# A two-block language-model kernel: gates with the activations stationary, the causal convolution in strips on TensorE, states in parts, and first loads on three queues beside matmuls on a tile of ones

## The chip, the core and the metric

The kernel runs on one core of a Trainium2 chip. The metric is the time of one execution on the device, in microseconds (us). Engines are named as in the profile: PE is TensorE (PEld its weight loads), DVE is VectorE, ACT is ScalarE, POOL is GpSimd and SP is SyncE, which only issues transfers here. SPq and ACTq are what these engines' sequencers do, mostly issuing DMAs.

## The reference

The input is one sequence of 256 tokens, width 1024, in float32. It passes four layers.

- Two hybrid layers. Each takes `z = rmsnorm(x) @ w_in` and splits it into a sliding-window attention (8 heads), a chunked retention (4 heads, with its own gate `rg`) and two output gates:

```python
ya = sliding_window_sink_attention(aq, ak, av, sinks) @ w_a
yb = (r * silu(rg)) @ w_b                      # r: the normed retention
mixed = jax.nn.sigmoid(ga) * ya + jax.nn.sigmoid(gb) * yb
x = x + mixed @ w_out
x = x + jnp.square(jax.nn.relu(rmsnorm(x) @ w_up)) @ w_down
```

- An even layer: block attention beside a multi-scale pooling, gated, then an output projection.
- An odd layer: an S5 state-space model (32 groups, 64 states) beside a gated convolution:

```python
g = a * jax.nn.sigmoid(gl)
c = causal depthwise convolution of g, 31 taps, 512 channels
conv_out = (silu(layernorm(c)) @ pw) * silu(gd)
return jnp.concatenate([ssm_out, conv_out], axis=-1) @ w_out
```

## The kernel before

**Weights.** All weight matrices are cut into chunks of 128 x 2048 numbers (1 MB) and packed in the order in which they are used. `fetch` issues the load of a chunk on SP into one of three `raw` buffers. ACT copies it to `hi` (rounded to fp32r), DVE computes `lo = raw - hi`; each half chunk of 1024 columns has its own `hi` and `lo`, five buffers of each. `chunk()` keeps two chunks prepared ahead. An activation is likewise held as a pair (`xh`, `xl`), and a product is three matmuls: hi x hi, hi x lo, lo x hi.

**Two forms of a projection.** `n_group` keeps a 128-token block of the activation stationary and streams 512 columns of weights; the result has tokens on the partitions. A group of 512 output columns takes two chunks of 24 matmuls. `t_pair` and `t_quad` keep 128 x 128 weights stationary and stream 256 tokens; the result has channels on the partitions, and a chunk takes 48 matmuls. Before, the queries, keys, values and `rg` use `n_group`; the output gates (`gate`), `ya`, `yb` and `xo` use `t_pair` or `t_quad`. `R = row(r)` spreads the token norms along the free axis for the gates.

**The mixer.** `gate` multiplies by `R` on DVE and takes tanh on ACT. Attention and retention steps are written between the gates. After `ya` and `yb`, each pair of row blocks is added up on DVE and split into `mh`, `ml`, which the matmuls of `xo` read.

**The odd layer.** The gated input `g` has channels on the partitions, four blocks of 128 (q = 0 to 3), with 30 columns of zeros ahead of the 256 tokens. `NPE = (0, 0, 23, 31)` says how many of the 31 taps of a block are done on PE, as matmuls with a diagonal matrix (`cdg`, made on ACT; results in `cq`); the others are multiply-adds of 128 x 256 on DVE (line 1317). `states(q)` turns the inputs of the state-space model (`vb`, in the four `sm` banks of PSUM) into states by rotations with `E`, two scans and rotations back, on DVE. `s5_outputs` copies the powers `pwc` into `Q`. `ys` then makes the model's outputs, with 32 output columns per matmul in four column groups. `layer_mean` (`mu`) needs the complete convolution `cv`; `gb` and `ga` are the products with `glu_w`, `pw` that of the convolution's branch, `yo` the last projection.

**What sets the order.** Each engine works off its own instructions in order. The order is made at build time by a list scheduler, which goes by the order in the program and its own model of durations; `tc.high_priority(-n)` moves what it holds back by about n instructions. A tile that takes over the place of another (same tag) waits until the last reader of the old one is done, wherever that stands in the program.

**The start.** SP issues, in this order, a first piece of chunk 0, the gains `pv`, `x` pair 0, and then pieces and pairs in turn. The first chunk is split in pieces of 512 columns.

Of the kernel before, what the change touches and what calls it, by code (L numbers as in the profile page):

```python
# [32 lines left out]
P = 128  # L33
D = 1024
# [11 lines left out]
LOWC, LOWS, LOWW, LOWX = 400, 1500, 250, 300  # L46

NPE = (0, 0, 23, 31)
# [8 lines left out]
def _layer_chunks(l):  # L57
# [7 lines left out]
    def nform(cols):  # L65
        for c in range(2):
            cs.append([("w_in", l, np.arange(k * P, k * P + P), cols) for k in range(4 * c, 4 * c + 4)])
# [88 lines left out]
def pack_weights(cs, inp):  # L156
# [3 lines left out]
    for blocks, n in zip(cs, w):  # L160
# [17 lines left out]
       ("glub", 8), ("dw", 4 * CONVK), ("lng", 4), ("lnb", 4), ("sinks", 16)]  # L178
# [8 lines left out]

def pack_vectors(inp):
    def v(a):
        return np.asarray(a, np.float32).reshape(-1, P).T  # L190

    cols = [v(inp["g_mix"]), v(inp["g_mlp"]), v(inp["g_final"]), v(inp["pre_norm_g_2"]), v(inp["post_norm_g_2"]),
            v(inp["e_pool_scale_2"]), v(inp["o_d_2"]), v(inp["o_glu_b_2"]),
            inp["o_dw_2"][0].reshape(CONVK, 4, P).transpose(2, 1, 0).reshape(P, 4 * CONVK),
            v(inp["o_ln_g_2"]), v(inp["o_ln_b_2"]),
            np.broadcast_to(inp["sinks"].reshape(1, 16), (P, 16))]
    return np.ascontiguousarray(np.concatenate(cols, axis=1))
# [16 lines left out]
_CT = [("ident", 128), ("mask0", 128), ("maske", 256), ("ecos", 64), ("esin", 64), ("blk", 128), ("icnt", 64)]  # L214
# [11 lines left out]
def tables():  # L226
# [42 lines left out]
    put("blk", blk)  # L269
    return t  # L270
# [5 lines left out]
def build(ctx, tc, w, xin, pv_in, ct_in, s5_in, pg_in, out, parts=(0, 1, "e", "o"), dbg=None):  # L276
# [33 lines left out]
    def fetch(pieces=None):  # L310
# [10 lines left out]
        for h in range(0, n, HW):  # L321
            hi = stream.tile([P, HW], F32R, name=f"hi{i}_{h}", tag="hi", bufs=NH)
            lo = stream.tile([P, HW], F32R, name=f"lo{i}_{h}", tag="lo", bufs=NH)
            m = min(HW, n - h)
            step = m if pieces is None else 512
            for c in range(0, m, step):
                s, rs = slice(c, c + step), slice(h + c, h + c + step)
                if pieces is not None:
                    nc.sync.dma_start(raw[:, rs], src[:, rs])
                    pieces((h + c) // 512)  # L330
                A.copy(hi[:, s], raw[:, rs])  # L331
                V.tensor_tensor(lo[:, s], raw[:, rs], hi[:, s].bitcast(F32), op=OP.subtract)  # L332
            his.append(hi)
            los.append(lo)
# [54 lines left out]

    def n_group(xh, xl, width=512, hook=None):  # L390

        b = [bank("acc", f"ng{t}") for t in range(NT)]
        if width == 512:
            for c in range(2):
                hi, lo = chunk()
                if c and hook:
                    hook()
                for kk in range(4):
                    k = 4 * c + kk
                    ws = slice(kk * 512, kk * 512 + 512)  # L400
                    for t in range(NT):
                        ts = slice(t * P, t * P + P)
                        f, e = k == 0, k == KT - 1
                        T.matmul(b[t], xh[:, k, ts], hi[:, ws], start=f, stop=False)  # L404
                        T.matmul(b[t], xh[:, k, ts], lo[:, ws], start=False, stop=False)  # L405
                        T.matmul(b[t], xl[:, k, ts], hi[:, ws], start=False, stop=e)  # L406
# [195 lines left out]
    def layer(l, xh, xl, norm, after_mixer, done):  # L602
# [37 lines left out]
        R = row(r)  # L640
# [101 lines left out]
        ga, gb = (phase[0].tile([P, KT, S], F32, name=n, tag="gate", bufs=2) for n in ("ga", "gb"))  # L742
# [47 lines left out]
        n2 = Norm(D)  # L790
        for p in range(4):
            b = t_pair("acc", "xo", mh, ml)
# [231 lines left out]
    def s5_scalars(pool, tmp):  # L1024
# [119 lines left out]
        pwc = pool.tile([P, 2 * L, 16, 16], F32, name="pwc")  # L1144
# [83 lines left out]
    def odd(pool, xh, xl, n, s5, tabs5):  # L1228
# [31 lines left out]
        def states(q):  # L1260
# [10 lines left out]
            m = pool.tile([P, 4, NC], F32, name="Mt", tag="Mt", bufs=1)  # L1271
            V.tensor_copy(m, mL[:, 4 * q:4 * q + 4, None].to_broadcast([P, 4, NC]))
            V.memset(m[:, :, 0:1], 0.0)
# [10 lines left out]
        GW = CONVK - 1 + S  # L1284
# [4 lines left out]
        V.memset(g[:, :, 0:CONVK - 1], 0.0)  # L1289

        def tap(q, k):
            return vec("dw", q * CONVK + k)

        for p in range(2):
# [7 lines left out]
            stt(g[:, 2 * p:2 * p + 2, CONVK - 1:], th, 1.0, a1, AD, M)  # L1302
# [7 lines left out]
            with tc.high_priority(-LOWC):  # L1310
                for q in (2 * p, 2 * p + 1):
                    for k in range(NPE[q], CONVK):
                        src = g[:, q, k:k + S]
                        if k == NPE[q]:
                            ts(cv[:, q, :], src, tap(q, k), None, M)
                        else:
                            stt(cv[:, q, :], src, tap(q, k), cv[:, q, :], M, AD)
# [4 lines left out]
        for q in range(4):  # L1322
            if NPE[q] == 0:
                continue
            b = bank("sm", "cq")
            for k in range(NPE[q]):
                dg = pool.tile([P, P], F32, name="cdg", tag="cdg", bufs=7)
                A.activation(dg, ident, AF.Copy, scale=tap(q, k))
                T.matmul(b[:, 0:S], dg, g[:, q, k:k + S], start=k == 0, stop=k == NPE[q] - 1)
            if NPE[q] == CONVK:  # L1330
                A.copy(cv[:, q, :], b[:, 0:S])
            else:
                with tc.high_priority(-LOWC):
                    tt(cv[:, q, :], cv[:, q, :], b[:, 0:S], AD)
# [150 lines left out]

    def x_pair(i):

        if i == 0:
            nc.sync.dma_start(pv[:, 0:NG], pv_in[:, 0:NG])
        if i in (0, 2, 4, 6):  # L1490
            p = i // 2
            nc.sync.dma_start(x[:, 2 * p:2 * p + 2, :], xin[:, 2 * p:2 * p + 2, :])
            split_pair(xh, xl, x, "g_mix", 0, p)
# [127 lines left out]
```

## Time and profile before

| | |
|---|---|
| median of 3 runs | 1061.71 us (1060.48 to 1061.8) |
| profiled execution | 1061.03 us, span 1059.2 us |
| busy in the span | PE 98%, PEld 88%, DVE 75%, ACT 53%, POOL 1% |
| mean granted PE clock | 0.997 of full speed |
| HBM read | 174.80 MB, 166 GB/s over the span |

The span runs from the first to the last instruction of the profiled execution; what is left of its time lies outside. Matmuls are pipelined, so an instruction's duration is longer than the interval to the next one. An fp32 matmul or transpose shows as two records. In a row of the timeline the bracket says how long the engine was idle before, and what it waited for.

### The profile page before, as it was taken

The page shows a single profiled execution, that of the slowest core. Times are in us where ns is not written, and L with a number is a line of the kernel's source. Part 1 is how long each engine was busy: PE and PEld are TensorE (multiplying, and loading weights), DVE is VectorE, ACT ScalarE, POOL GpSimd, SP SyncE. Part 2 cuts the span into 40 slices and gives each one's busy share as a digit, 9 for nine tenths or more (in the row PEclk, how much of TensorE's full clock was granted, in tenths as well). Part 3 has the DMA queues.
Part 4 walks back from the last instruction along what each step waited for, and adds up shares of the span by engine and source line. Part 5 has one row for each costly group of instructions (what it writes and reads, how often), then busy time and mean ns, then how long its engine had stood idle before and what let it go on. Part 6 is the DMA issues. An engine that isn't in the chain of part 4 may idle for free.

```text
span 1059.2 us, 17142 instructions
## 1 busy us (share of the span) xinstructions
PE 1037.1 (98%) x6904; PEld 927.1 (88%) x6904; DVE 791.6 (75%) x1402; ACT 564.1 (53%) x895; POOL 9.4 (1%) x10
## 2 busy tenths in 40 slices
PE   7999999999999999999999999999999999999996
PEld 5888999998888887888999988888878999999885
DVE  6767666786666659568656799976668795989985
ACT  6545644555454546446444554444466558465453
POOL 0000000000000000000000000000000001010000
PEclk9999999999999999999999999999999999999999
DMA  9654434555555455553535555555544354334021
GB/s 330 224 178 159 160 118 162 182 182 199 194 188 197 171 199 168 190 177 106 195 120 178 202 199 169 204 185 196 201 160 159 129 200 160 120 125 175 2 80 40
DMA packets 26719, 176.95 MB, mean 167 GB/s; under 512 B 3088, under 2 KB 3216, under 8 KB 6032
## 3 DMA queue, kind: packets, MB, share of 16 engines
q1 hardware_dynamic: 26064, 174.26, 47.5%
q0 software_dynamic: 288, 1.07, 0.3%
q8 instruction: 54, 0.88, 0.3%
q10 hardware_dynamic: 288, 0.52, 0.1%
q14 instruction: 25, 0.20, 0.1%
HBM read 174.80 MB, written 1.05 MB: 166 GB/s over the span
## 4 chain that ended last, share of the span: by engine, by line
PE 90%; DVE 6%; ACT 2%; issue 1%; DMA 0%; SPq 0%; DVEq 0%; ACTq 0%
PE up L810 11%; PE ng L406 6%; PE ng L404 6%; PE ng L405 6%; PE up L811 6%; PE dn L832 5%; PE dn L833 5%; PE dn L834 5%; PE gate L386 3%; PE gate L387 3%; PE gate L388 3%; DVE big L1019 2%; PE xo L386 1%; PE xo L387 1%; PE yb L388 1%; PE yb L386 1%
## 5 line engine op out<-in xcount | busy, mean ns | idle before, releaser
L332 DVE TENSOR_TENSOR lo<-raw,hi 128x1024 fp32r<-128x1024 f32 (+1 forms) x331 | 398.1, 1208 | 177.3 <-ACT hi L331 176.2
L331 ACT CAST hi<-raw 128x1024 fp32r<-128x1024 f32 (+1 forms) x331 | 341.6, 1038 | 307.5 <-PE dn L834 83.2
L810 PE MATMUL up<-xs,hi 128*128 128x512 f32 x512 | 181.9, 398 | 0.0
L811 PE MATMUL up<-xs,lo 128*128 128x256 f32 x512 | 143.5, 280 | 0.0
L810 PEld LDWEIGHTS up<-xs,hi 128*128 128x128 f32 x512 | 96.2, 188 | 23.3
L404 PE MATMUL ng<-hi,xs 128*128 128x512 f32 x272 | 108.4, 399 | 8.1 <-ACT xs L455 8.1
L405 PE MATMUL ng<-lo,xs 128*128 128x512 f32 x272 | 107.2, 394 | 0.0
L406 PE MATMUL ng<-hi,xs 128*128 128x512 f32 x272 | 106.8, 395 | 0.1
L832 PE MATMUL dn<-hi,uph 128*128 128x512 f32 x256 | 100.1, 391 | 0.0
L833 PE MATMUL dn<-lo,uph 128*128 128x512 f32 x256 | 99.9, 390 | 0.0
L834 PE MATMUL dn<-hi,upl 128*128 128x512 f32 x256 | 99.6, 389 | 0.0
L811 PEld LDWEIGHTS up<-xs,lo 128*128 128x128 f32 x512 | 96.6, 189 | 1.0
L386 PE MATMUL gate<-xs,hi 128*128 128x256 f32 x256 | 74.0, 289 | 0.0
L388 PE MATMUL gate<-xs,lo 128*128 128x256 f32 x256 | 72.4, 283 | 0.0
L387 PE MATMUL gate<-xs,hi 128*128 128x256 f32 x256 | 72.4, 283 | 0.0
L404 PEld LDWEIGHTS ng<-hi,xs 128*128 128x128 f32 x272 | 51.7, 190 | 18.9 <-ACT xs L455 8.6
L406 PEld LDWEIGHTS ng<-hi,xs 128*128 128x128 f32 x272 | 51.4, 190 | 11.8 <-DVE xs L456 1.0
L405 PEld LDWEIGHTS ng<-lo,xs 128*128 128x128 f32 x272 | 51.7, 190 | 10.5
L832 PEld LDWEIGHTS dn<-hi,uph 128*128 128x128 f32 x256 | 48.1, 188 | 10.5
L834 PEld LDWEIGHTS dn<-hi,upl 128*128 128x128 f32 x256 | 48.1, 188 | 10.2
L833 PEld LDWEIGHTS dn<-lo,uph 128*128 128x128 f32 x256 | 48.1, 188 | 8.9
L386 PEld LDWEIGHTS gate<-xs,hi 128*128 128x128 f32 x256 | 49.0, 191 | 2.4 <-issue 2.3
(384 smaller groups left out, 2128.9 us busy)
## 6 DMA issues: line engine op xcount, KB each, us to landing
raw<-w_dram SPq DMA_DIRECT2D x161, 1024.0 KB, 4.9
raw<-w_dram SPq DMA_DIRECT2D x9, 256.0 KB, 5.8
x<-x_dram SPq DMA_DIRECT2D x4, 256.0 KB, 5.9
ctm<-ct_dram SPq DMA_DIRECT2D x1, 640.0 KB, 10.1
sp<-s_dram POOLq DMA_DIRECT2D x1, 536.0 KB, 3.9
pg<-pg_dram POOLq DMA_DIRECT2D x1, 512.0 KB, 3.9
out_dram<-xn SPq DMA_DIRECT2D x2, 256.0 KB, 2.0
out_dram<-xn ACTq DMA_DIRECT2D x2, 256.0 KB, 2.1
```

Of the source, the lines that this page charges most:

```text
L331: A.copy(hi[:, s], raw[:, rs])
L332: V.tensor_tensor(lo[:, s], raw[:, rs], hi[:, s].bitcast(F32), op=OP.subtract)
L386: T.matmul(o, wh, xh, start=first, stop=False, skip_group_check=True)
L387: T.matmul(o, wh, xl, start=False, stop=False, skip_group_check=True)
L404: T.matmul(b[t], xh[:, k, ts], hi[:, ws], start=f, stop=False)
L405: T.matmul(b[t], xh[:, k, ts], lo[:, ws], start=False, stop=False)
L406: T.matmul(b[t], xl[:, k, ts], hi[:, ws], start=False, stop=e)
L810: T.matmul(bs[i], hi[:, ws], xs2[:, k], start=k == 0, stop=False, skip_group_check=True)
L811: T.matmul(bs[i][:, 1, :], lo[:, ws], xh2[:, k, :], start=False, stop=k == KT - 1, skip_group_check=True)
L832: T.matmul(accs[t][h], th[:, kk, tk], hi[:, ws], start=f, stop=False)
L833: T.matmul(accs[t][h], th[:, kk, tk], lo[:, ws], start=False, stop=False)
L834: T.matmul(accs[t][h], tl[:, kk, tk], hi[:, ws], start=False, stop=e)
```

## The change

1. In the two hybrid layers the gates, `ya` and `yb` use the form of `n_group`, through a new `n_half` that does one chunk. Their results have tokens on the partitions, so the norm is ACT's scale and `R` is dropped. The sum of the two branches is turned to channels by 16 transposes a layer (`mixed`). The first `xo` pair runs over row blocks in its outer loop.
2. The convolution is done on PE alone. `strip` copies `g`, 32 channels at a time, into `g4` by 16 DMAs for each pair of blocks: the partitions of one strip hold 32 channels at four shifts of 8 tokens. A matmul with 32 output columns then does four taps at once; `taps` builds its matrices on POOL. There are 8 x 4 matmuls for each block. `g4` takes the places of `pwc` and `E`.
3. `states` is called in four places, a mask copy in it moves from DVE to ACT and the memsets to POOL.
4. `x` is loaded from ACT's queue, the first part of `pv` from POOL's, the weights alone from SP's. DVE makes the first `hi`. PE does 12 matmuls on the tile of ones before its first work.

```diff
-LOWC, LOWS, LOWW, LOWX = 400, 1500, 250, 300
-NPE = (0, 0, 23, 31)
+LOWS, LOWW, LOWX = 1500, 250, 300
+NIDLE = 12
+KP = 8
...
-    for p in range(4):
-        pair("w_in", ga + 256 * p)
-    for p in range(4):
-        pair("w_in", gb + 256 * p)
+    for c0 in (ga, ga + 512, gb, gb + 512):
+        nform(np.arange(c0, c0 + 512))
...
-    for p in range(4):
-        pair("w_b", 256 * p)
+    for c0 in (0, 512):
+        nform(np.arange(c0, c0 + 512), "w_b")
...
-                A.copy(hi[:, s], raw[:, rs])
+                if pieces is not None and i + h + c == 0:
+                    V.tensor_copy(hi[:, s], raw[:, rs])
+                else:
+                    A.copy(hi[:, s], raw[:, rs])
...
+    def n_half(b, xh, xl, c, nk=KT):
+        hi, lo = chunk()
+        for kk in range(4):
+            k = 4 * c + kk
+            ws = slice(kk * 512, kk * 512 + 512)
+            for t in range(NT):
+                ts = slice(t * P, t * P + P)
+                f, e = k == 0, k == nk - 1
+                T.matmul(b[t], xh[:, k, ts], hi[:, ws], start=f, stop=False)
+                T.matmul(b[t], xh[:, k, ts], lo[:, ws], start=False, stop=False)
+                T.matmul(b[t], xl[:, k, ts], hi[:, ws], start=False, stop=e)
...
-        R = row(r)
...
-        def gate(o, p):
-            b = t_pair("acc", "gate", xh, xl)
-            s = o[:, 2 * p:2 * p + 2, :]
-            V.tensor_tensor(s, b, row2(R), op=OP.mult)
-            A.activation(s, s, AF.Tanh, scale=0.5)
+        def gate(o, i):
+            c = i // 2
+            if i % 2 == 0:
+                gates["b"] = [bank("acc", f"gate{t}") for t in range(NT)]
+            n_half(gates["b"], xh, xl, i % 2)
+            if i % 2:
+                for t in range(NT):
+                    A.activation(o[:, t, c * 512:c * 512 + 512], gates["b"][t], AF.Tanh, scale=rc(0, t))
...
         for c in range(2):
-            for p, b in enumerate(t_quad("acc", "ya", oTh, oTl)):
-                s = ga[:, 4 * c + 2 * p:4 * c + 2 * p + 2, :]
-                V.scalar_tensor_tensor(s, s, 1.0, b, op0=OP.add, op1=OP.mult)
+            cs = slice(c * 512, c * 512 + 512)
+            bs = [bank("acc", f"ya{t}") for t in range(NT)]
+            n_half(bs, oTh, oTl, 0, 4)
+            for t in range(NT):
+                V.scalar_tensor_tensor(ga[:, t, cs], ga[:, t, cs], 1.0, bs[t], op0=OP.add, op1=OP.mult)
         mh, ml, ms = twin("ms")
-        for p in range(4):
-            b = t_pair("acc", "yb", rTh, rTl)
-            s = gb[:, 2 * p:2 * p + 2, :]
-            V.scalar_tensor_tensor(s, s, 1.0, b, op0=OP.add, op1=OP.mult)
-            V.tensor_tensor(s, s, ga[:, 2 * p:2 * p + 2, :], op=OP.add)
-            split(mh[:, 2 * p:2 * p + 2, :], ml[:, 2 * p:2 * p + 2, :], s)
+        def mixed(c):
+            for t in range(NT):
+                b = bank("sm", "mt").rearrange("p (n q) -> p n q", q=P)
+                for n in range(4):
+                    k = 4 * c + n
+                    T.transpose(b[:, n, :], gb[:, t, k * P:k * P + P], ident)
+                tk = slice(t * P, t * P + P)
+                split(mh[:, 4 * c:4 * c + 4, tk], ml[:, 4 * c:4 * c + 4, tk], b)
+        for c in range(2):
+            cs = slice(c * 512, c * 512 + 512)
+            bs = [bank("acc", f"yb{t}") for t in range(NT)]
+            n_half(bs, rTh, rTl, 0)
+            if c:
+                mixed(0)
+            n_half(bs, rTh, rTl, 1)
+            for t in range(NT):
+                s = gb[:, t, cs]
+                V.scalar_tensor_tensor(s, s, 1.0, bs[t], op0=OP.add, op1=OP.mult)
+                V.tensor_tensor(s, s, ga[:, t, cs], op=OP.add)
+        mixed(1)
...
-            b = t_pair("acc", "xo", mh, ml)
+            b = t_pair("acc", "xo", mh, ml, k_outer=p == 0)
...
+        def strip(p):
+            g4[p] = s5["pool"].tile([P, 2, 4, GS + 1], F32, name="g4", tag=("pwc", "E")[p], bufs=1)
+            for s in range(4):
+                for r in range(4):
+                    nc.sync.dma_start(g4[p][32 * s:32 * s + 32, :, r, 0:GS],
+                                      g[32 * r:32 * r + 32, 2 * p:2 * p + 2, KP * s:KP * s + GS])
+        def taps(q, h):
+            n = 2 * KP
+            o = PVO["dw"] + (2 * q + h) * n
+            tap[q, h] = pool.tile([P, n, 32], F32, name="taps", tag="taps", bufs=3)
+            G.tensor_tensor(tap[q, h], pv[:, o:o + n, None].to_broadcast([P, n, 32]),
+                            C("e32")[:, None, :].to_broadcast([P, n, 32]), op=M)
+        def convolve(p):
+            b = bank("sm", "cq").rearrange("p (j t) -> p j t", j=2)
+            for j in range(2):
+                q = 2 * p + j
+                for k in range(KP):
+                    if k % 4 == 0:
+                        taps(q, k // 4)
+                    for r in range(4):
+                        T.matmul(b[32 * r:32 * r + 32, j, :], tap[q, k // 4][:, 4 * (k % 4) + r, :],
+                                 g4[p][:, j, r, k:k + S], start=k == 0, stop=k == KP - 1)
+            A.copy(cv[:, 2 * p:2 * p + 2, :], b)
...
+            strip(p)
             if p == 0:
                 inputs()
                 with tc.high_priority(-LOWW):
-                    for q in range(4):
-                        states(q)
                     Q = s5_outputs(pool, s5)
...
-        for d in (gc, gd):
+        for i, d in enumerate((gc, gd)):
+            with tc.high_priority(-LOWW):
+                states(i)
             for p in range(2):
                 silu_gate(d[:, 2 * p:2 * p + 2, :], t_pair("acc", "og", xh, xl), R, 0.25)
...
+        convolve(0)
+        states(2)
+        convolve(1)
+        states(3)
...
+    nc.gpsimd.dma_start(pv[:, 0:NG], pv_in[:, 0:NG])
+    for p in range(4):
+        nc.scalar.dma_start(x[:, 2 * p:2 * p + 2, :], xin[:, 2 * p:2 * p + 2, :])
+    idle = bank("sm", "idle")
+    for _ in range(NIDLE):
+        T.matmul(idle[:, 0:P], ones, ones, start=True, stop=True)
```

## Rows read from the trace of the kernel before

**Rows 1.** The page's part 4, the chain that ended last, by engine.

```profile
PE 90%; DVE 6%; ACT 2%; issue 1%; DMA 0%; SPq 0%; DVEq 0%; ACTq 0%
```

**Rows 2.** Windows, busy us (x instructions) of PE, PEld, DVE, ACT, POOL; clock, DMA.

```profile
995.00:1008.00 13.00, 10.26 (x293) 8.91 (x293) 12.98 (x30) 0.62 (x1) 0.00 (x0) 1.00 0.01 3
```

**Rows 3.** Timeline of PE, odd layer: start, us, what, [idle before <- releaser].

```profile
996.50 1.97 PE L1368 MATMUL ys<-wall,Q 128*32 128x63 f32 x128
...
1002.85 1.36 PE L1348 MATMUL mu<-big,ones 128*128 128x256 f32 x4
1006.95 1.13 PE L1348 MATMUL mu<-big,ones 128*128 128x256 f32 x4 [2.74 <-DVE big L1010]
...
1035.35 0.36 PE L387 MATMUL pw<-is__10046,hi 128*128 128x256 f32 x1
```

**Rows 4.** Timeline of all engines, the first 21 us.

```profile
0.73 1.28 ACT L331 ACT_TABLE_LOAD   x1 [0.73 <-PEq L1611]
...
0.84 0.17 DVE L349 MEMSET ones<- 128x128 f32 x1 [0.84 <-PEq L1611]
...
1.65 0.42 SPq L1492 DMA_DIRECT2D x<-x_dram  x1
...
6.71 0.91 ACT L455 ACTIVATE xs<-x,pv 128x256 fp32r<-128x256 f32 x2 [1.95 <-DMA x<-x_dram]
...
7.27 0.80 PE L404 MATMUL ng<-hi,xs 128*128 128x512 f32 x1 [7.27 <-ACT xs L455]
...
13.58 0.40 PE L406 MATMUL ng<-hi,xs 128*128 128x512 f32 x1
...
20.40 0.39 PE L406 MATMUL ng<-hi,xs 128*128 128x512 f32 x1
```

**Rows 5.** The chain in order of time: start, us on the chain, what.

```profile
11.91 0.43 PE ng L405
...
32.18 0.87 PE tp L560 x8
...
66.62 0.45 PE rb L534 x4
...
100.50 0.12 PE gate L386
...
104.09 0.12 PE gate L386
```

**Rows 6.** Timeline at the end of the first mixer.

```profile
194.90 0.28 PE L388 MATMUL yb<-rTs,lo 128*128 128x256 f32 x1
...
199.04 0.69 DVE L450 TENSOR_TENSOR ms<-gb,ms 128x512 fp32r<-128x512 f32 x1 [0.69 <-ACT ms L449]
```

**Rows 7.** Windows of the start (last columns: clock, DMA share, GB/s).

```profile
0.00:7.20 7.20, 0.00 (x0) 0.00 (x0) 0.86 (x2) 2.39 (x4) 0.21 (x4) 1.00 0.63 145
7.20:12.10 4.90, 4.83 (x11) 3.84 (x12) 4.34 (x8) 4.65 (x11) 0.00 (x0) 1.00 1.00 351
```

**Rows 8.** DMA issues: count, KB each, median us from issue to landing.

```profile
raw<-w_dram SPq DMA_DIRECT2D x161, 1024.0 KB, 4.9
...
sp<-s_dram POOLq DMA_DIRECT2D x1, 536.0 KB, 3.9
...
out_dram<-xn SPq DMA_DIRECT2D x2, 256.0 KB, 2.0
```

**Rows 9.** The tile `cq`: durations in ns, first and last start.

```profile
L1329 PE MATMUL cq<-big,cdg x108: 377/378/380, 970.7 to 993.8; 128*128 128x256 f32 x108
```

**Rows 10.** Timelines of POOL, ACT and DVE in the odd layer.

```profile
937.49 3.57 POOL L1221 MEMSET Q<- 128x2048 f32 x2
...
950.24 0.41 ACT L1175 ACTIVATE Q<-pwc 64x256 f32<-64x256 f32 x1
...
978.76 0.42 DVE L1019 SCALAR_TENSOR_TENSOR wall<-wall,tb 128x256 f32<-128x256 f32 x1
...
979.75 18.29 DVE L1019 SCALAR_TENSOR_TENSOR big<-big,pv 128x256 f32<-128x256 f32 x46
```

More of the change, by code (lines that the diff above doesn't have):

```diff
@@ L63, in _layer_chunks, with nform @@
                             for b in range(4)])
-    def nform(cols):
+    def nform(cols, name="w_in"):
         for c in range(2):
-            cs.append([("w_in", l, np.arange(k * P, k * P + P), cols) for k in range(4 * c, 4 * c + 4)])
+            cs.append([(name, l, np.arange(k * P, k * P + P), cols) for k in range(4 * c, 4 * c + 4)])
     def pair(name, c0, n=1024):
@@ L185, with strips @@
 NG = 16
+def strips(dw):
+    t = np.zeros((4 * KP, 512), np.float32)
+    t[:CONVK] = dw
+    return t.reshape(4, KP, 4, 4, 32).transpose(0, 4, 2, 1, 3).reshape(P, 16 * KP)
 def pack_vectors(inp):
@@ L193, in pack_vectors @@
             v(inp["e_pool_scale_2"]), v(inp["o_d_2"]), v(inp["o_glu_b_2"]),
-            inp["o_dw_2"][0].reshape(CONVK, 4, P).transpose(2, 1, 0).reshape(P, 4 * CONVK),
+            strips(inp["o_dw_2"][0]),
             v(inp["o_ln_g_2"]), v(inp["o_ln_b_2"]),
@@ L269, in tables @@
     put("blk", blk)
+    put("e32", np.tile(np.eye(32), (4, 1)))
     return t
@@ L393, in n_group @@
         if width == 512:
[L394 to L406, printed above, removed]
+            n_half(b, xh, xl, 0)
+            if hook:
+                hook()
+            n_half(b, xh, xl, 1)
         else:
@@ L739, in ret_flip @@
                 split(rTh[:, 4 * c:4 * c + 4, tk], rTl[:, 4 * c:4 * c + 4, tk], b)
-        ga, gb = (phase[0].tile([P, KT, S], F32, name=n, tag="gate", bufs=2) for n in ("ga", "gb"))
-        def gate(o, p):
-            b = t_pair("acc", "gate", xh, xl)
-            s = o[:, 2 * p:2 * p + 2, :]
-            V.tensor_tensor(s, b, row2(R), op=OP.mult)
-            A.activation(s, s, AF.Tanh, scale=0.5)
+        ga, gb = (phase[0].tile([P, NT, D], F32, name=n, tag="gate", bufs=2) for n in ("ga", "gb"))
+        gates = {}
+        def gate(o, i):
[6 more added lines that the diff above has]
+                    A.activation(o[:, t, c * 512:c * 512 + 512], gates["b"][t], AF.Tanh, scale=rc(0, t))
         ret_gate(0)
@@ L1143, in s5_scalars @@
         pwb = pool.tile([P, 2 * L, 16, 16], F32, name="pwb", tag="pwb", bufs=1)
-        pwc = pool.tile([P, 2 * L, 16, 16], F32, name="pwc")
+        pwc = pool.tile([P, 2 * L, 16, 16], F32, name="pwc", tag="pwc", bufs=1)
         for pw, src, first in ((pwb, 0, (fr, fi)), (pwc, 2, (ar, ai))):
@@ L1270, in states @@
             tt(wt[:, 1], wt[:, 1], tb[:, 0], SU)
-            m = pool.tile([P, 4, NC], F32, name="Mt", tag="Mt", bufs=1)
-            V.tensor_copy(m, mL[:, 4 * q:4 * q + 4, None].to_broadcast([P, 4, NC]))
-            V.memset(m[:, :, 0:1], 0.0)
+            m = w2("Mt")[:, 0:4 * NC].rearrange("p (r c) -> p r c", r=4)
+            A.copy(m, mL[:, 4 * q:4 * q + 4, None].to_broadcast([P, 4, NC]))
+            G.memset(m[:, :, 0:1], 0.0)
             mf = m.rearrange("p r c -> p (r c)")
@@ L1281, in states @@
             stt(wt[:, 1], wt[:, 1], -1.0, tb[:, 0], M, SU)
-        GW = CONVK - 1 + S
+        GW = 4 * KP + S
         big = pool.tile([P, 4 * (GW + 3 * S)], F32, name="big", tag="big", bufs=1)
@@ L1288, in odd @@
                       for i in range(3))
-        V.memset(g[:, :, 0:CONVK - 1], 0.0)
-        def tap(q, k):
-            return vec("dw", q * CONVK + k)
+        G.memset(g[:, :, 0:CONVK - 1], 0.0)
+        G.memset(g[:, :, CONVK - 1 + S:], 0.0)
+        GS = S + KP - 1
+        g4, tap = {}, {}
+        def strip(p):
[21 more added lines that the diff above has]
+            A.copy(cv[:, 2 * p:2 * p + 2, :], b)
         for p in range(2):
@@ L1305, in odd @@
                 with tc.high_priority(-LOWW):
-                    for q in range(4):
-                        states(q)
                     Q = s5_outputs(pool, s5)
                 G.dma_start(pg, bass.AP(tensor=pg_in.tensor, offset=pg_in.offset, ap=[[0, P], [1, D]]))
[L1310 to L1317, printed above, removed]
-        for d in (gc, gd):
+        for i, d in enumerate((gc, gd)):
+            with tc.high_priority(-LOWW):
+                states(i)
             for p in range(2):
                 silu_gate(d[:, 2 * p:2 * p + 2, :], t_pair("acc", "og", xh, xl), R, 0.25)
[L1322 to L1334, printed above, removed]
+        convolve(0)
+        states(2)
+        convolve(1)
+        states(3)
         fh, fl, fs = twin("fs")
```

12 lines of the change are left out of this document (4 added, 8 removed).

## The prediction

> **What bounds the kernel now.** I read the page's chain first, then the windows, then the timeline and the chain where they leave TensorE. PE holds 90% of the chain, DVE 6% [rows 1]: a microsecond taken out of PE's queue is one off the time wherever PE does not wait. The windows show where it does: from 995 to 1008 DVE is full and PE is not [rows 2]. PE's timeline names that wait, 2.74 us before the second part of the mean over channels (`mu`), for DVE, which still has taps of the convolution to do [rows 3]. The other place is the start: nothing runs on PE for 7.27 us [rows 4], and the matmuls after it come at half pace. So there are three stretches, each with its own sum, against the profiled execution: a span of 1059.2 us and a time of 1061.0, 0.7 under the median of 1061.7.
>
> **The two mixer layers.** Gates, `ya` and `yb` change from 48 matmuls of 256 columns to 24 of 512 for each 1 MB chunk of weights. In a gate 30 intervals between matmuls take 3.59 us, 0.1197 each [rows 5]; in an `n_group`, the form they change to, 30 intervals take 6.82 us (13.58 to 20.40), 0.2273 each [rows 4]. A chunk falls from 48 x 0.1197 = 5.75 to 24 x 0.2273 = 5.46 us, 0.29 less. There are 16 gate chunks, 4 of `ya` and 8 of `yb`: 28 x 0.29 = 8.2 us. The row `R` of each layer goes: 2 x 0.45 = 0.9 us [rows 5]. What is added is `mixed`: 16 transposes a layer. One transpose is two records; eight records take 0.87 us [rows 5], so one takes 0.217 and 32 take 7.0 us. Net 8.2 + 0.9 - 7.0 = 2.1 us of PE work saved.
>
> DVE loses eight 128x512 multiplications a layer, and ACT's tanh reads PSUM instead; neither ends a wait of PE there, so I count nothing. The splits stay as many.
>
> The transposes also lengthen the last chain of the mixer. Now the last `yb` matmul starts at 194.90 and the last subtraction behind it ends at 199.73, 4.6 us after the matmul's end [rows 6]; PE does `xo` matmuls meanwhile and loses about half a microsecond. After, there are two more DVE operations of 0.69 us, four transposes (0.87) and one more handover: some 2.4 us more, 7.0 us. Token tile 0 ends 0.7 us earlier, the 24 `xo` matmuls of the first four row blocks cover 2.9, and the eight transposes are work themselves (1.7): at most 1.7 us stays, nothing if matmuls of the next `xo` pair are drawn ahead, and the old half microsecond goes. I take 0.5 a layer. If PE keeps the written order (transposes ahead of `xo`), it idles for four DVE operations less the 0.7, and a weight's `lo` (some 1.2) among them: 3.3 us a layer. Layers: 2.1 - 1.0 = **1.1 us saved**, between 2.1 saved and 4.5 lost.
>
> **The start.** Now `x` pair 0 is issued at 1.65, behind a weight piece and `pv` on SP; the activation that waits for it begins at 6.71, the first matmul at 7.27 [rows 4]. After, it is first on ACT's queue, at about 0.74, where the table load stands now. That load (1.28 us) follows the four issues and is over by 3.7: nothing waits for it. With the same 5 us to land, the activation begins near 5.7 and a matmul near 6.2. The tile of ones is ready at 1.0 [rows 4]. Twelve fp32 matmuls of 128 columns take 12 x 0.217 x 1.89 = 4.9 us at the slow pace and end at 6.1: no obstacle. 1.89 is the ratio of a 512-column interval early, 0.43 us [rows 5], to 0.2273 later: the 1.2 GHz level after an idle stretch against 2.4, though the windows' clock column reads 1.00 [rows 7]. PE reached the higher level 4.9 us after its first matmul. If it does so again, the real ones start fast near 6.1, and about 11 of them save 0.2 us each, 2.3 in all. Earlier start and clock: 1.1 + 2.3 = 3.4 us.
>
> Then supply: from 7.2 to 12.1 the DMA engines are full at 351 GB/s, but before 7.2 they moved 145 [rows 7]. If they are full from 2.7 us on, (7.2 - 2.7) x 0.351 = 1.58 MB land by 7.2 instead of 1.04: 0.54 MB, 1.5 us earlier. So the start gives between 1.5 (all supply) and 3.4 us; nothing is seen of PE waiting for weights there, so it has some slack, and I take **2.8 us**. POOL's issue of `pv` is not shown; the nearest row, `sp` on POOL, lands 3.9 us after issue [rows 8], before `x`.
>
> The Trainium skill ("DMA: Bandwidth & Descriptors", section "Issuing engines are not separate DMA queues") speaks against this part: transfers issued from several engines share the same 16 DMA engines, and only issue time is saved. The full engines of [rows 7] agree; if supply alone counts, the start gives the 1.5 us and the total is 1047.8.
>
> **The convolution.** Now 54 diagonal matmuls (108 records, first start 970.7, last 993.8) take 0.216 us a record, 0.432 a matmul, 23.3 us in all [rows 9]; DVE does the other 70 taps at 0.40 us, 28 us [rows 10]. After, PE does everything in 128 matmuls of 32 output columns each, in four column groups. Their cost is the largest unknown. If the groups overlap fully, one costs 0.432 / 4 = 0.108 and all 13.8 us. The nearest row is `ys`, also fp32, 32 columns wide and in four groups: 128 records take 1.97 us [rows 3], less the last one's own 0.22, 0.0138 each, 0.0276 a matmul of 63 moving columns. A wide one would take 0.432 x 63/256 = 0.106, so the overlap is 3.85-fold. Scaled to 256 columns that is 0.112 and 14.4 us. I take 14.2: 9.1 us off PE. From above: no overlap, 0.432 each and 55.3 us.
>
> The Trainium skill ("TensorE: Matmul & The Clock Gate", Part 3 on packing small matmuls) gives less: 2.38-fold for three column groups. An estimate at that share for four is 3.17-fold, 17.4 us for the convolution and 1049.7 in the sum; the 3.85 of `ys` is better than that.
>
> With the taps gone the wait before `mu` goes: 2.74 us, 3.0 with the drained pipe. What is late next? The strips. Those of pair 1 take `E`'s place and so wait for the last of the four `states`, which ends on DVE at 979.2 now [rows 10]. Seven taps that lie before it (2.8 us) and its copies and memsets (about 1 us) are gone, so about 975. Sixteen issues on SP at 0.42 us [rows 4] and a landing of 2.0 (the output's, [rows 8]) give 983.7. PE comes to the second half of the convolution at 970.7 + 7.1 = 977.8, or after `ys` (8.8 us, from 994 to 1002.85 in [rows 3]) at 986.6. If the convolution is put first, it waits up to 5.9 us; if `ys`, nothing. I take 1.5. The strips of pair 0 wait for the last read of `pwc`, by the `Q` copies that end at 950.7 [rows 10]; PE needs them 20 us later. Weights queue behind these 32 issues on SP, 6.7 us a pair; they are issued some two chunks, 11 us, ahead and land in 4.9 [rows 8], so this is hidden. Without that cover it costs up to 5 us. POOL builds eight tap tiles of 512 elements: two memsets of 2048 take it 3.57 us [rows 10], so 0.45 us from below and, with two inputs beside the output, 1.4 from above; PE uses a tile for 16 x 0.111 = 1.8 us, and three are ready ahead. Nothing.
>
> The chain from `mu` to the second half of `pw` (1007 to 1035 in [rows 3]) is as long as PE's work beside it: it moves with `mu` and is not shortened. Odd block: 9.1 + 3.0 - 1.5 = **10.6 us**.
>
> Sum: 1.1 + 2.8 + 10.6 = 14.5; 1061.0 - 14.5 = **1046.5 us**.
>
> **The rivals.** (1) *Late handovers.* PE waits for strips (5.9 instead of 1.5) or keeps the written order in the layers (6.6 instead of 1.0): 1050.9 or 1052.1, both 1056.5; a held-up weight queue is of the same size. For it: PE takes its queue in an order fixed ahead of the run. Against: before [rows 6]'s subtraction ended, `xo` matmuls had already been drawn ahead. (2) *Partial overlap.* With the groups overlapping three-fold, 55.3 / 3 = 18.4 us: 1050.7. Two by two, 0.216 a matmul and 27.6 us, 4.3 more than now: 1061.0 + 4.3 - 3.0 + 1.5 - 3.9 = 1059.9. Against: `ys`. (3) *No overlap,* the slower side: 55.3 us, 32.0 more, and no time lost to strips: 1061.0 + 32.0 - 3.0 - 3.9 = 1086.1. It decides from (23.3 + 3.0 + 3.9) / 128 = 0.236 us a matmul on. For it: no row has 256 columns in a 32-column group. (4) *Supply,* three queues that give only their earlier start: 1047.8.
>
> **How the numbers follow.** Forecast 0.42; (4) 0.18: both within the forecast's own range, 1041 to 1050. (1) 0.22 and three-fold overlap 0.05, 1050 to 1057. Two by two 0.05. (3) 0.05. Something unseen 0.03, most of it slower. The range 1040 to 1057 leaves out about 0.13. A change under 0.2% (2.1 us) can't be told from none, and two by two lies on that edge: same 0.05, faster 0.88, slower 0.07.
>
> **What would show it.** Right: the first 512-column matmul near 6.2 us and 0.23 us apart; gate chunks of 5.46 us; `cq` records 0.055 us apart on average and no wait for DVE before `mu`; `gb` near 995. Wrong: `cq` records at 0.1 or more; a gap before the second half of `cq`; PE idle between the last `yb` and `xo`; PE waiting for weights near 17 to 24 us.

## The result and the profile after

The changed kernel takes 1068.83 us (median of 4 runs) beside 1061.1 us of the kernel before on the same chip. The ratio is 1.0071, with an interval of 1.0052 to 1.0089: slower, where 1046.5 was forecast and the range ended at 1057. The profiled execution has a span of 1066.4 us [before: 1059.2] and a mean granted clock of 0.985 [0.997].

The page's chain has become purer: VectorE's share falls from 6% to 2% [rows 1]. But a share says what ends last, not how long it takes.

```profile
PE 93%; DVE 2%; ACT 2%; issue 1%; DMA 1%; SPq 1%; DVEq 0%; ACTq 0%; POOLq 0%
```

The first landmarks show where to look. Matmuls of a given tile start, after less before: the first transposes -0.2 us, the second layer -2.9, the even layer's `pu` -4.5, the first diagonal or packed convolution matmul -1.4, the first `gb` +7.4. So the loss lies in the odd block: 3.1 us between `pu` and the convolution and 8.8 between its first half and `gb`. The windows of the second stretch stand beside [rows 2]: the wait for VectorE that stood in 995 to 1008 is gone, and 21 us ahead of it TensorE is busy for 3.

```profile
974.00:995.00 21.00, 3.16 (x51) 1.55 (x41) 11.10 (x16) 0.59 (x1) 4.07 (x3) 0.65 0.32 95
995.00:1008.00 13.00, 13.00 (x203) 8.04 (x205) 0.00 (x0) 0.59 (x1) 1.06 (x1) 0.90 0.03 7
```

TensorE's timeline (beside [rows 3] and [rows 9]) names the wait: the second half of the convolution waits 17.84 us for the strips of pair 1. It then starts at a granted clock of 0.50 (994.3 to 996 us), the 1.2 GHz level; over the two windows above it is 0.65 and 0.90.

```profile
969.29 7.14 PE L1353 MATMUL cq<-g,taps 128*32 128x256 f32 x128
994.27 1.65 PE L1353 MATMUL cq<-g,taps 128*32 128x256 f32 x4 [17.84 <-DMA g<-big]
...
998.32 7.11 PE L1353 MATMUL cq<-g,taps 128*32 128x256 f32 x122
...
1013.50 1.99 PE L1394 MATMUL mu<-big,ones 128*128 128x256 f32 x8
```

The timelines of SP and VectorE (beside [rows 10]) show why the strips are late. SP issues those of pair 0 from 949.20, and those of pair 1 only from 984.43, 0.03 us after VectorE's last product that reads `E`. Each 16 issues take 10.2 to 11.1 us, 0.64 to 0.69 each.

```profile
949.20 11.08 SPq L1335 DMA_DIRECT2D g<-big  x16
984.43 10.17 SPq L1335 DMA_DIRECT2D g<-big  x16
...
973.74 2.92 DVE L1312 TENSOR_TENSOR_SCAN wall<-Mt,wall 128x256 f32<-128x256 f32 x2
983.71 0.69 DVE L1046 TENSOR_TENSOR wall<-wall,E 128x512 f32<-128x512 f32 x1
984.78 0.42 DVE L1055 SCALAR_TENSOR_TENSOR wall<-wall,tb 128x256 f32<-128x256 f32 x1
```

At the start (beside [rows 4]) the four `x` issues stand at 0.74 on ScalarE's queue, but the first real matmul comes at 7.87, 0.6 later than before. The table load waits until `x` has landed, and the activation behind it then waits for `pv`, which GpSimd's queue delivers at 7.3. The ones matmuls end at 5.52; after the 2.35 us without work the real ones run 0.42 apart, and the window that stands beside [rows 7] has a clock of 0.65.

```profile
0.74 2.13 ACTq L1535 DMA_DIRECT2D x<-x_dram  x4
1.06 4.46 PE L1538 MATMUL idle<-ones 128*128 128x128 f32 x24 [1.06 <-DVE ones L358]
1.24 0.72 POOL L1533 DMA_DIRECT2D pv<-pv_dram  x1 [0.79 <-POOLq L1660]
5.32 1.28 ACT L468 ACT_TABLE_LOAD   x1 [5.32 <-DMA x<-x_dram]
7.31 0.91 ACT L468 ACTIVATE xs<-x,pv 128x256 fp32r<-128x256 f32 x2 [0.70 <-DMA pv<-pv_dram]
7.87 0.79 PE L408 MATMUL ng<-hi,xs 128*128 128x512 f32 x1 [2.35 <-ACT xs L468]
```

```profile
7.20:12.10 4.90, 4.23 (x12) 3.37 (x13) 4.23 (x9) 4.79 (x11) 0.00 (x0) 0.65 1.07 401
```

One more place stood in no plan. At the entry of the odd block TensorE runs dry twice in the short matmuls of `kb`, with nothing to wait for ("issue"), and `su` starts at 0.21 us a matmul instead of 0.12, at a granted clock of 0.50 from 902 to 904 us, the 1.2 GHz level. From the first `kb` matmul to the first `cb` matmul behind `su` it takes 12.29 us, before 8.24: 4.05 us are lost here.

```profile
895.50 1.30 PE L1241 MATMUL kb<-cd,BA 128*32 128x32 f32 x128
898.01 1.29 PE L1241 MATMUL kb<-cd,BA 128*32 128x32 f32 x128 [1.22 <-issue]
902.01 0.37 PE L395 MATMUL su<-xs,hi 128*128 128x256 f32 x1 [2.72 <-issue]
```

### The profile page after: what moved, and what is told of

It reads as the page before. It is cut to its first block, busy times and chain, and to the rows that moved or that the text cites. A ratio compares the mean times of both kernels' runs of the same rounds, so it can differ in the third digit from the quotient of the medians.

```text
span 1066.4 us, 16107 instructions
## 1 busy us (share of the span) xinstructions
PE 1029.9 (97%) x6428; PEld 887.8 (83%) x6428; DVE 760.1 (71%) x1307; ACT 546.6 (51%) x843; POOL 23.3 (2%) x25
## 3 DMA queue, kind: packets, MB, share of 16 engines
HBM read 174.82 MB, written 1.05 MB: 165 GB/s over the span
## 4 chain that ended last, share of the span: by engine, by line
PE 93%; DVE 2%; ACT 2%; issue 1%; DMA 1%; SPq 1%; DVEq 0%; ACTq 0%; POOLq 0%
PE up L846 11%; PE ng L410 6%; PE ng L408 6%; PE ng L409 6%; PE up L847 6%; PE dn L869 5%; PE dn L868 5%; PE dn L870 5%; PE gate L408 3%; PE gate L409 3%; PE gate L410 3%; PE xo L395 1%; PE xo L397 1%; PE xo L396 1%; PE yb L409 1%; PE yb L410 1%
## 5 line engine op out<-in xcount | busy, mean ns | idle before, releaser
L870 PEld LDWEIGHTS dn<-hi,upl 128*128 128x128 f32 x256 | 48.1, 188 | 10.2
L408 PE MATMUL gate<-hi,xs 128*128 128x512 f32 x128 | 51.6, 403 | 0.0
L410 PE MATMUL gate<-hi,xs 128*128 128x512 f32 x128 | 49.9, 390 | 0.0
L409 PE MATMUL gate<-lo,xs 128*128 128x512 f32 x128 | 49.9, 390 | 0.0
L854 ACT COPY upa<-up 128x256 f32<-128x256 f32 x64 | 23.7, 370 | 47.8 <-PE up L847 47.8
```

The costliest lines, as they stand in the source:

```text
L854: A.copy(u[:, j, :], b[:, 0, :])
L870: T.matmul(accs[t][h], tl[:, kk, tk], hi[:, ws], start=False, stop=e)
```

## The experiments

Ratios below are to the kernel before on the same chip, each with its 95% interval. The changed kernel was timed on one chip, the others on four more, where the kernel before took 1061.5 to 1063.0 us: a difference to the changed kernel's 1068.83 is good to a microsecond or two. Four theories were put to the chip. (1) The strips of pair 1 wait for the tile `E`, which the last `states` free late. (2) TensorE's instructions arrive in pieces, and the ones matmuls shift the piece ends to a bad place in `kb`. (3) GpSimd's tap products slow VectorE and so delay the states. (4) At the start, `pv`, the table and the gap ahead of the first real matmul take back what the queues give.

**Another place for the second strips.** The tile goes into the ring of weight buffers instead of the place of `E`.

```diff
-            g4[p] = s5["pool"].tile([P, 2, 4, GS + 1], F32, name="g4", tag=("pwc", "E")[p], bufs=1)
+            if p == 0:
+                g4[p] = s5["pool"].tile([P, 2, 4, GS + 1], F32, name="g4", tag="pwc", bufs=1)
+            else:
+                g4[p] = stream.tile([P, 8 * (GS + 1)], F32, name="g4", tag="raw", bufs=3).rearrange(
+                    "p (j r t) -> p j r t", j=2, r=4)
```

> The second strip tile takes a slot of the weight stream's raw ring instead of the tile E, so it no longer waits for the last part of the states. Theory 1, the strips' wait sets the loss: their 16 issues follow the first 16 directly (about 960 to 971), land by 973, the second half of the convolution follows the first at 976.4, and the skip and state matmuls wait only for the states (985); the wait of 17.8 us and the slow clock behind it shrink to about 8, and the run takes 1068.8 - 10 to 17, 1052 to 1059. Rival A, VectorE's late states set the loss: TensorE stops at 983.6 and waits for the states all the same, and of the 17.8 us at most 7 come back, 1062 to 1066. Rival B, a ring with one slot less starves the weights: no gain, and waits of the matmuls on weight tiles instead.

Measured: 1057.93 us, ratio 0.9951 (0.9931 to 0.9972): 10.9 us less than the changed kernel, as theory 1 has it, at the lower end. Rival A, that TensorE would wait for the states all the same, falls. SP issues all 32 strips in one row and TensorE waits 3.1 us for them in all.

```profile
946.32 21.92 SPq L1339 DMA_DIRECT2D g<-big  x32
```

But the fixed order changed with the tile: the convolution now stands ahead of half of the `og` gates, and so nearer to its strips. From 965 to 970 TensorE is busy for 2.88 of 5 us; the 2.12 us it lacks are its longest wait for strips. Part of the price stays.

**The second half last.** Only the place of one call.

```diff
         states(2)
-        convolve(1)
         states(3)
...
             if p == 1:
+                convolve(1)
                 nv = layer_mean()
```

> Only the order on TensorE: the second half of the convolution is emitted behind the skip and state matmuls, just ahead of the mean. Theory 1: these start when the last states end (985) instead of at 1005, fill the wait for the strips, and the second half follows from 994 or so at 7.1 us: the mean comes about 9 us earlier than 1013.5, 1068.8 - 9 = 1060. If the states rather than the strips hold TensorE, the same matmuls wait for them and the gain is under 4 us, 1065 or more.

Measured: 1057.68 us, 0.9956 (0.994 to 0.9972), 11 us less. The strips are issued as late as before (984.20), but the `ys` matmuls start at 976.13, those that read the states at 978.67, and with a part of `gb` and `ga` they fill the wait; 2.1 us of it are left. The gain is more than the 9 that were expected. Order and lateness are two handles on one loss.

```profile
PE cq L1353 <- DMA g<-big: 2.1, 1, 2.1
PE gb L395 <- ACT is__9274 L462: 0.8, 1, 0.8
```

**Each other part alone.** The kernel before, with the layers' part and with the start's.

> The kernel before with the layers' part of the change alone (gates, branch outputs, transposes). By the trace of the changed kernel, whose second layer ended its mixer 4.5 us earlier, it takes 1061.1 - 4.3 = 1056.8. By the prediction's sum it is 1.1 us faster, 1060.0.

> The kernel before with the changed start alone (three queues, matmuls on the tile of ones, first cast on VectorE). By the trace of the changed kernel, whose first transposes came 0.2 us earlier, no difference: 1060.9. By the prediction's sum 2.8 us faster, 1058.3.

Measured: layers alone 1058.84 us, 0.9977 (0.9959 to 0.9996), 2.4 us faster and between the two expectations; start alone 1064.84 us, 1.0026 (1.0009 to 1.0042), 2.8 us slower, against both expectations. In its profile the first transposes come 1.6 us earlier than before, and this lead holds to 898 us. There it is lost, and 2.2 us more by the first `cb` matmul, in code that is the same in both kernels:

```profile
898.16 1.25 PE L1209 MATMUL kb<-cd,BA 128*32 128x32 f32 x123
900.41 1.31 PE L1209 MATMUL kb<-cd,BA 128*32 128x32 f32 x128 [1.00 <-issue]
904.41 0.33 PE L1209 MATMUL kb<-cd,BA 128*32 128x32 f32 x5 [2.69 <-issue]
```

The counts matter: 123, then 128. In the kernel before there is one gap of 1.05 us, behind record 148. The only TensorE instructions that this kernel adds are the 12 ones matmuls, 24 records, at its very start. This gave theory 2.

**Where the instruction pieces end.** Fewer ones matmuls, and, in another kernel, half of `kb` behind `su`.

```diff
-NIDLE = 12
+NIDLE = 4
```

> The changed kernel with 4 matmuls on the tile of ones instead of 12. Theory 2, TensorE's instruction stream is fetched in pieces, and the short matmuls of kb run through two piece ends: 8 matmuls fewer (each two passes) move the ends by some 17 of kb's 128-wide groups, the first to about 144, the second out of kb into the longer su matmuls, where it is hidden. The gap of 2.7 us ahead of su and the slow clock behind it go, some 3.5 us; the start may lose up to 2 us if the clock is then granted later. 1064 to 1067. If the gaps belong to that place of the program, whatever stands ahead of it, two gaps stay and the run takes 1068.8 to 1071.

```diff
         sus = [t_pair("acc", "su", xh, xl, k_outer=p == 0) for p in range(2)]
+        inner((2, 3))
...
             inner((0, 1))
-            inner((2, 3))
```

> The second half of kb's short matmuls is emitted behind the su matmuls instead of ahead of them, so no 256 of them stand in one row. Theory 2 (instruction supply): TensorE no longer runs dry ahead of su; su starts when its operands are ready, about 3 us earlier, and at full clock: 1068.8 - 3 to 5, 1064 to 1066. If su waits for its operands and the gap only shows as missing instructions, no gain: 1068.8.

Measured: 1064.79 us, 1.0033 (1.002 to 1.0046), and 1065.27 us, 1.0032 (1.0021 to 1.0044): both some 4 us under the changed kernel, as theory 2 said. From the first `kb` to the first `cb` matmul their profiles take 8.70 and 8.73 us instead of 12.29, so the gain lies at that place; the split's profile is also 1.4 us ahead at the first transposes, with the same code there. With 4 ones matmuls the first gap stands behind record 144, the very place named, and the second has left `kb` (0.6 us inside `su`):

```profile
895.33 1.43 PE L1241 MATMUL kb<-cd,BA 128*32 128x32 f32 x144
897.64 1.15 PE L1241 MATMUL kb<-cd,BA 128*32 128x32 f32 x112 [0.89 <-issue]
```

The record behind which the first gap comes, by kernel: before 148 and with the start alone 123; layers alone 153, the changed kernel with 4 ones matmuls 144, with 12 of them 128. From no ones matmuls to 4 it is 9 records, to 12 it is 25: two for each, and one more. Two runs below, with 16 and 20, have it behind 120 and 112: 33 and 41. The pages and the transfer views bear this out. The changed kernel's page has 50 packets on the instruction queue q8, for 2 x 6428 TensorE instructions (each matmul record has a weight load): 257 to a packet. The kernel before has 54 for 2 x 6904: 256, the 128 records between two gaps. That q8 serves TensorE is read from this fit.

```profile
PE 1029.9 (97%) x6428; PEld 887.8 (83%) x6428; DVE 760.1 (71%) x1307; ACT 546.6 (51%) x843; POOL 23.3 (2%) x25
...
q8 instruction: 50, 0.82, 0.3%
```

In the changed kernel packets of this queue stand at 895.1 and 899.1 us, and the two gaps end at 898.01 and 902.01. In 13 profiles all 20 gaps at `kb` and `su` end 2.2 to 2.9 us behind such a packet, also two that the wait list puts down to ScalarE's `sq` (in the runs with the second half last and with the states early). What holds up the packets themselves is open.

**One tap tile.** GpSimd builds one of the eight, which serves all eight places; the products for the other seven are left out.

```diff
+            if tap:
+                tap[q, h] = tap[0, 0]
+                return
             tap[q, h] = pool.tile([P, n, 32], F32, name="taps", tag="taps", bufs=3)
```

> One tap tile, built once, serves all eight places, so GpSimd's other seven multiplications are left out (the convolution then uses the wrong taps). Theory 3, GpSimd's multiplications slow VectorE's work beside them: scans of 1.27 us that took 2.92 and products of 0.68 that took 1.53 go back, the last states end some 4 us before 985, the strips and all behind them come 4 us earlier: 1064.8. If they cost nothing on the path, 1068.8; what TensorE waits for the strips stays at 13 us or more in either case.

Measured: 1064.65 us, 1.0026 (1.0009 to 1.0042), just as theory 3 said. The two scans that took 2.92 us take 1.27, the last `states` operation starts at 981.35 instead of 984.78, and the wait for the strips falls by as much:

```profile
972.81 1.27 DVE L1312 TENSOR_TENSOR_SCAN wall<-Mt,wall 128x256 f32<-128x256 f32 x2
...
981.35 0.42 DVE L1055 SCALAR_TENSOR_TENSOR wall<-wall,tb 128x256 f32<-128x256 f32 x1
```

```profile
PE cq L1356 <- DMA g<-big: 14.5, 1, 14.5
```

So theory 3 holds as a part, 3.3 of the 17.8 us; the rest is when the states are issued.

**The states where they were.** The edit goes back on one point of the change alone.

```diff
                 with tc.high_priority(-LOWW):
+                    for q in range(4):
+                        states(q)
                     Q = s5_outputs(pool, s5)
...
-            with tc.high_priority(-LOWW):
-                states(i)
...
         convolve(0)
-        states(2)
         convolve(1)
-        states(3)
```

> Only the place of the states: all four parts are again emitted right behind their inputs, as in the kernel before, instead of two ahead of the gates, one behind each half of the convolution. Theory 1 says that the strips wait because the last states, which free the tile E, are late: with them done by about 960 to 965 the second strips' issues end by 975, the second half follows the first, the wait of 17.8 us falls to under 3 and the run takes about 1068.8 - 14 to 18, 1051 to 1055. If early states only push VectorE's other work (gates, splits) behind, the gates' matmuls wait on weights instead and less than 8 us come back, over 1061.

Measured: 1047.11 us, 0.9868 (0.9845 to 0.9892): 21.7 us less, where 14 to 18 were expected, and 0.6 from the forecast of 1046.5. In the changed kernel the first scan ran at 950.94; here the first two run from 932.79, `E` is free at 964.49, and SP issues the second strips at 964.52.

```profile
966.86 7.14 PE L1353 MATMUL cq<-g,taps 128*32 128x256 f32 x128
975.33 0.59 PE L1353 MATMUL cq<-g,taps 128*32 128x256 f32 x2 [1.33 <-POOL taps L1342]
...
979.72 7.10 PE L1353 MATMUL cq<-g,taps 128*32 128x256 f32 x122
...
993.46 1.99 PE L1392 MATMUL mu<-big,ones 128*128 128x256 f32 x8
```

The wait for strips is gone from TensorE's list; what stays in this stretch is 1.33 us for a tap tile. The mean comes at 993.46, 20.0 us before the changed kernel's: 16.5 of it are the wait, 1.1 the clock behind it, and 2.4 stand ahead of the convolution, most of them at `kb` (10.43 us to the first `cb` instead of 12.29), whose code the edit leaves as it was. Nothing shows that these 2.4 come from the states.

**Both repairs, and two more.** Early states with the split `kb`; then, on top of it, another start; then, instead of that start, the second half of the convolution last; and that one with 20 ones matmuls.

> Early states and the second half of kb behind su, together. If the two losses are separate (strips late, instruction supply at kb), their gains add: 1047.1 - 3.6 = 1043.5. If the early states already hide what kb costs, no more than 1047.1 - 1.

> As the run before, with another start: the first columns of pv go out on ScalarE's queue behind the first piece of x instead of on GpSimd's, one activation of a column of ones brings ScalarE's table in ahead of x, and 16 instead of 12 matmuls on the tile of ones reach up to the first real one. Theory 4, in the changed kernel pv's landing (7.3) and the table load behind x set the first activation (7.3), and the gap of 2.35 us ahead of the first real matmul lets TensorE's clock go: the first activation comes at about 5.5, the first real matmul at about 6.1, at full clock, and the first transposes 1.5 to 2 us earlier than 31.8: 2 us better than the run before. If the weights set the start from there on, the transposes come at 30.3 to 31 and 1 us or less is left.

> As the first of these, with the second half of the convolution behind the skip and state matmuls. The second strips and tap tiles then have 6 us more; the wait of 1.3 us for a tap tile and the stretch in which strips still land go: 1.3 to 2 us better than the first. If the layer mean, which now follows the second half directly, leaves TensorE waiting for the copy of the result (0.6 us and a handover), the gain is 0 to 1.

> As the run with the second half last, with 20 matmuls on the tile of ones instead of 12. Theory 4, the idle stretch ahead of the first real matmul decides whether TensorE's clock holds: in the profiles so far idle stretches of 1.34 to 1.64 us were followed by a granted clock of 1.00 (transposes at 30.2 to 30.7), stretches of 1.77 to 2.67 by 0.50 (31.7 to 32.5), with the same code. With 20 the stretch is under 1.2, the clock holds in every execution, the transposes come at 30.2 to 30.7, and the time is that of the faster executions of the run before, 1043.5 to 1044.4. If the longer row delays the first real matmul (past 7.9), 1044.4 to 1045.5.

Measured, in this order: 1046.68 us, 0.9853 (0.9828 to 0.9878); 1045.58, 0.9841 (0.982 to 0.9862); 1044.41, 0.9834 (0.981 to 0.9858); and 1046.15, 0.9842 (0.982 to 0.9865). The intervals overlap; what each edit did is read from the profiles.

The first missed its 1043.5. The two gains do not add: the run with early states alone had lost less at `kb` (a first gap of 0.31 us, and `su` at the full clock), so there was less to win: 1.8 us at that place (10.43 to 8.63), and the spans are 1046.2 and 1044.5. The second gained 1.1, under the 2 of theory 4. The table came no earlier: the queue of ScalarE was held by its own `x` issues until 6.06 (the bracket names the landing of `x`; which of the two it was is not separated), and the first real matmul stands at 8.04. What it has is the clock: 1.64 us without work ahead of it instead of 2.10, a granted clock of 1.00 behind it, and the first transposes at 30.7 instead of 32.0.

```profile
1.66 4.40 ACTq L1535 DMA_DIRECT2D x<-x_dram  x3
6.09 1.28 ACT L1537 ACT_TABLE_LOAD   x1 [6.09 <-DMA x<-x_dram]
7.49 0.89 ACT L468 ACTIVATE xs<-x,pv 128x256 fp32r<-128x256 f32 x2
```

The third is the fastest by its median, 1.7% under the kernel before and 2.3 us under the first, where 1.3 to 2 were expected. But its order did little of that. Its profile is 1.9 us ahead of the first one's already at the first transposes, with the same code there, and 2.2 ahead at `gb`:

```profile
L573 PE MATMUL tp<-ct,rqn x8: 272/272/273, 32.0 to 33.3; 128*128 128x128 f32 x8
L395 PE MATMUL gb<-is__9348,hi x16: 279/283/467, 993.4 to 999.2; 128*128 128x256 f32 x16
...
L573 PE MATMUL tp<-ct,rqn x8: 270/272/273, 30.2 to 31.4; 128*128 128x128 f32 x8
L395 PE MATMUL gb<-is__9274,hi x16: 283/283/466, 991.2 to 996.8; 128*128 128x256 f32 x16
...
PE ys L1412 <- issue: 1.8, 1, 1.8
```

From the first `cq` to the first `gb` matmul the third takes 27.4 us and the first 27.9. The last line shows what took most of the gain: a gap of the kind seen at `kb` now stands in the short matmuls of `ys`, behind record 51 of the second run of 128, again 2.4 us behind a packet. With 20 ones matmuls it stands behind record 35, 16 earlier: two for each.

The fourth missed. Its clock did hold (10 matmuls from 9 to 11 us, at 1.00, where the changed kernel had 6 at 0.50), but the first transposes still came at 32.01, 1.8 us later than in the third: the first real matmul stands 0.4 later, and a wait of the norm's sums for VectorE had come in, which the third has not.

```profile
PE ss L508 <- DVE sqf L484: 1.1, 1, 1.1
```

This run agrees with the clock part of theory 4, its worth it does not show; the spread of this kernel's own runs (1044.3 to 1048.8) is larger than what was sought.

## Why the prediction was wrong

**The failed step** is the answer to "What is late next? The strips." The mechanism was named, and its price was off by a factor of twelve: 1.5 us taken, 5.9 as the worst, 17.84 measured, and a slow clock behind it. Three numbers went wrong together. The states were said to end at about 975, with nothing counted for calling them in four places; they ended at 985.2, because the change issues them in four parts (the first scan at 950.94 instead of 932.79 in the run that puts them back) and because tap products run beside them (3.4 us, where the sum has "Nothing." for these products). The issue was priced at 0.42 us from a transfer of `x`; these took 0.64, 10.2 us instead of 6.7. And TensorE's row was taken to be free to put `ys` in front; the row has `cq` first, so all of `ys` waited too. Against the worst case of 5.9 us, the tile came free 9.4 later, the issues took 3.5 longer and TensorE was there 1.4 earlier; some 2.3 came back, since the matmuls start before the last strip is issued (994.27 and 994.60). Rival 1 had this mechanism with its price of 5.9, so that the range ended too low and the slower side got 0.07. Early states alone give 1047.1 us, 0.6 from the forecast, but partly by luck: errors cancel. At `pu` that run is 4.4 us ahead of the kernel before, where 3.9 was said for layers and start, with the one put too low and the other too high; from `cb` to `gb` it gains 9.8 of the 10.6; and it loses 2.2 at `kb`, which no term had.

**The convolution's cost** was right. 128 records in 7.14 us are 0.0558 each, 0.1116 a matmul (0.111 said), against 0.432 [rows 9]: 3.87-fold. The estimate of 3.17-fold that was worked out from the Trainium skill ("TensorE: Matmul & The Clock Gate", Part 3 on packing small matmuls) is not borne out here; `ys` was the better guide, and partial and no overlap are excluded.

**The wait ahead of `mu`** went, as said: no wait for VectorE stands there.

**The layers** gave more than 1.1 us in their own stretch: `pu` starts 4.5 us earlier, 0.2 of it from the start. The mis-sized term is the transposes. One is one record, not two as was read: 16 records a layer (the tile view below), four in 0.39 us (193.22 to the next matmul at 193.61), 3.1 us in all instead of 7.0; and no stall shows ahead of `xo`, where 1.0 was counted. Then 8.2 + 0.9 - 3.1 = 6.0 is the bound, and 4.3 came. At the first `up` matmul of the second layer it is still 5.3; a little later, at 607.5, stands a new wait of 0.8 us for the split of `xs`, which the kernel before has not. Alone, the part's profile has `mu` 4.0 us and its end 3.3 us earlier, with a `kb` gap of 1.51 us; its median is 2.4 lower, and the rest was not traced.

```profile
L809 PE MATMUL mt<-ct,gb x16: 272/273/301, 185.2 to 194.2; 128*128 128x128 f32 x16
...
PE up L846 <- DVE xs L469: 0.8, 1, 0.8
```

**The start** was to give 2.8 us and gave 0.2. "Lands 3.9 us after issue, before `x`" failed: `pv` lands 6.0 us after its issue on GpSimd's queue. "Nothing waits for it" failed for the table load. And the clock was not kept: the ones matmuls left 2.35 us open. Over the runs with 12 of them the same code went both ways: gaps of 1.34 to 1.48 us and full clock behind them in four profiles (transposes at 30.2 to 30.4), gaps of 1.77 to 2.67 and a clock of 0.50, the 1.2 GHz level, in the others (31.8 to 32.5). The ones matmuls ended at 6.4 to 6.5 in the four and at 5.5 to 6.1 in the others; what decides their end, and with it the gap, was not tried.

**Not foreseen at all:** the ones matmuls as a shift of the instruction stream 890 us later, some 4 us. It makes the start alone a loss.

The account of the whole, from the changed kernel's profile beside the one before: layers and start -4.5 up to `pu`, `kb` and `su` +4.1, from there to the convolution -1.0, from its first matmul to `gb` +8.8, which makes the +7.4 at `gb`. The parts alone, layers -2.4 and start +2.8, leave some +7.3 for the convolution's part; that is a difference, and that part was not run alone.

## What to carry to other kernels

When a tile takes the place of another, the price of the wait is set by the last reader of the old one: follow that reader through every move of the same change, and price the issues of the new transfers by their own kind. Ask what stands next in the waiting engine's row, for work behind a wait waits too. Before work is spread out to smooth a queue, look for who needs its last part.

## What the runs showed of the hardware

- A row of short matmuls can outrun its own instruction supply. In `kb` (256 matmul records 0.010 us apart, each with a weight load) a gap comes every 128 records, takes 0.2 to 2.7 us, ends 2.2 to 2.9 us behind a packet of the instruction queue, and moved by two records for each ones matmul put ahead. Gaps of this kind stand in `ys` too, 1.75 and 1.36 us in the last two runs.
- A GpSimd product of two SBUF operands and a VectorE operation with two inputs in SBUF slow each other: 128x512 on GpSimd took 1.04 to 2.06 us in the changed kernel (up to 3.56 in the first of the last four), two scans on VectorE 2.92 instead of 1.27. The Trainium skill ("SBUF — State Buffer", section "Summary: rules for kernel authors") says that of such a pair the second to be issued waits until the first is done; the rows agree that the two do not run side by side at full pace.

```profile
L1342 POOL TENSOR_TENSOR taps<-pv,ct x8: 1042/1668/2059, 873.1 to 1000.4; 128x512 f32<-128x512 f32 x8
```

- The 8 KB of `pv`, issued on GpSimd's queue at 1.24 us, took 6.0 us to land, where a later transfer of 536 KB on that queue took 3.9 [rows 8]. The queue alone does not explain it: issued on ScalarE's at 1.18 us they took 6.0 too, on SP's at 1.18 us in the kernel before 3.1.
